# A two-layer float32 decoder trunk: the down projection's halves one group later, silu rows in the squares' buffers, rstd later in the first group

## The chip, the cores and the metric

The kernel runs on one core of a Trainium2 chip. A core has five engines that work side by side, each through its own instruction queue in order: TensorE (PE in the profile, with its weight loads as PEld) multiplies matrices, VectorE (DVE) and ScalarE (ACT) do elementwise work, GpSimd (POOL) does some more of it, and SyncE (SP) issues most DMAs. They wait for one another by semaphores. SBUF holds what the engines work on, PSUM the accumulating products, in eight banks. The metric is the device time of one execution in microseconds (us); less is better.

## The reference

The input is one sequence of 512 positions with 1024 features, all in float32. There are two layers. Each adds to the residual first a mixer and then a gated feed-forward block (FFN), both behind an RMS norm, and a last RMS norm follows. Layer 0's mixer is a short gated convolution beside a causal pooling over windows; layer 1's is a gated spatial mixing in chunks of 128 positions. The change lies in the two FFNs, which compute

```
def rms_norm(x, g):
    y = x * lax.rsqrt(jnp.mean(x * x, axis=-1, keepdims=True) + EPS)
    return y * g

def gated_conv_ffn(x, w_gate, w_up, conv_w, conv_b, w_down):
    g = x @ w_gate                       # 512 x 2816
    g = causal_dwconv3(g, conv_w) + conv_b
    up = x @ w_up                        # 512 x 2816
    return (silu(g) * up) @ w_down       # 512 x 1024

h = h + gated_conv_ffn(rms_norm(h, norm_ffn[layer]), ...)
```

## The kernel before

**Numbers in two parts.** Every float32 operand of a product is split into a part `hi` rounded to TensorE's float32r and the remainder `lo`, and a product is three: hi·hi, hi·lo, lo·hi (`mm3`, line 153). `hi` is a ScalarE copy. `lo` is made in one of two ways: by a VectorE subtraction (`halves`, line 677, and `parts`, line 146), or by a ScalarE copy of the negated source followed by a DMA from GpSimd's queue that adds the source onto it, beside the ScalarE copy that makes `hi` (`summed`, line 136, and lines 654 to 656).

**The rows of the FFN.** The 2816 hidden features are 22 tiles of 128 (`NF`). `Ffn.hidden(f)` makes tiles f and f+1 of silu(gate)·up. This text calls that a group; f is 0, 2, ..., 20. Group 0 multiplies directly (`direct`, line 604): 8 input tiles times 4 outputs (two gate, two up), three products of 512 columns each, 96 in all. The others use a seven-product block scheme for each of gate and up (`both`, line 681): fourteen products of twelve matmuls with 256 columns, on sums of blocks of the input (`block_sums`, line 634: `t41` and `t23` for each of four pairs `kp` of input tiles) and sums of blocks of the weights (`s12`, `s34`). The products g5 and u5, third and fifth in order, read `s12g` and `s12u`; they have the names g_4e and u_4e for group 4. The source tiles `t` of the block sums and the weight sums share one tag, "sum", with three buffers.

After a group, VectorE and ScalarE take its products out of PSUM, run the three-tap convolution (`conv`, line 573), silu (`silu`, line 582) and the product with `up`. The two finished rows `s` lie in a tag "s" with three buffers until `act` (line 587) splits them into a_hi and a_lo, a tag with four buffers each, so four rows can be split at a time.

**The down projection.** It runs in parts of two rows (the first) and then four, and each part in two halves of 512 output features. A half is `group` (line 158) with four PSUM banks: with `tail=4` the loop over outputs is the outer one for the last four rows, which for a part of four is all of it, so that the banks finish one after another; with `tail=0` the loop over rows is the outer one and all four banks finish in the last twelve products. VectorE adds each bank to the residual (line 310 in layer 0, whose weights and results have the name d; line 1099 in layer 1, name dn). The last part of layer 1 is `last_down` (line 1117), with the final norm.

**The order.** The list `STEPS` (line 523) says which halves follow which group, and whether the group's rows are split before (`late` False) or after them:

```
STEPS = [(0, False, []), (2, False, [(0, 2, 0), (0, 2, 1)]), (4, False, [(2, 6, 0)])]
for f in range(6, NF - 2, 4):
    STEPS += [(f, True, [(f - 4, f, 1)]), (f + 2, False, [(f, f + 4, 0)])]
```

So the first half of rows 2 to 5 follows group 4 directly, whose rows it reads. The program's order is a wish only: the framework's planner lays out every engine's queue at compile time. It takes what is ready by its own estimate of durations, earlier in the program first, and gives out buffers and waits. It can put products of the next group between those of a half. Instructions marked `inorder` keep the order in which the program names them.

**The norm.** The FFN multiplies the residual without its rstd, and the rstd is applied later. `Norm.square` (line 204) squares each residual tile on ScalarE into a tag "sq" with two buffers, and GpSimd adds it to `ssq`. In group 0, `rstd_cols` (line 223: eight small products ssc on TensorE, then square root, reciprocal and one refining step) and `rstd_spread` (line 213: four transposes ssr) are placed by counting (i, j), input tile and output, in the loop of `direct`: the first before the products of (1, 2), the second before those of (2, 1) (lines 770 and 772). In layer 1 the same loop also transposes the residual in its first two input tiles (`turn_residual`, line 1087).

**Weights.** A weight tile of 512 KB goes by SyncE's queue into a tag "raw" with four buffers; its parts lie in the tags "whi" and "wlo" with six buffers each, shared by all products.

Of the kernel before, what the change touches and what calls it, by code (L numbers as in the profile page):

```python
# [8 lines left out]
F32 = mybir.dt.float32  # L9
# [6 lines left out]
P = 128  # L16
D = 1024
S = 512
NK = D // P
NT = S // P  # L20
FF = 2816
NF = FF // P
# [10 lines left out]
def tile_trunk(ctx: ExitStack, tc: tile.TileContext, x, norm_mix, norm_ffn, final_norm,  # L33
# [9 lines left out]
    tp = ctx.enter_context(tc.tile_pool(name="tp", bufs=2))  # L43
# [3 lines left out]
    def mm_bank(name):  # L47
        return ps_mm.tile([P, 512], F32, tag="mm", name=name)
# [47 lines left out]
    def params(layer, rows_):  # L96
        return params_fetch(layer, rows_, nc.sync)()
# [55 lines left out]
    def mm3(ps, lhs, rhs, start, stop):  # L153
        nc.tensor.matmul(ps, lhs[0], rhs[0], start=start, stop=False)  # L154
        nc.tensor.matmul(ps, lhs[0], rhs[1], start=False, stop=False)  # L155
        nc.tensor.matmul(ps, lhs[1], rhs[0], start=False, stop=stop)  # L156

    def group(name, outs, ks, lhs, rhs, tail, on_done, before=None, at_end=None, begun=None):

        start, banks = begun or (0, {})
        head = max(0, len(ks) - tail)
        order = [(i, j) for i in range(start, head) for j in outs]
        order += [(i, j) for j in outs for i in range(head, len(ks))]
        at = start - 1
        for i, j in order:
            if i > at and before is not None:
                before(ks[i])  # L170
            at = max(at, i)
            if j not in banks:
                banks[j] = mm_bank(f"{name}_{j}")
            mm3(banks[j], lhs(ks[i], j), rhs(ks[i], j), i == 0, i == len(ks) - 1)
            if i == len(ks) - 1 and at_end is None:
                on_done(j, banks[j])
        if at_end is not None:
            at_end()
            for j in outs:
                on_done(j, banks[j])  # L180
# [114 lines left out]
            chunks[k0], chunks[k0 + 1] = (hi, lo, 0), (hi, lo, 1)  # L295
        return chunks

    def project(name, w, acts, ks, norm, before=None, halves=(0, 1)):

        for gi in halves:  # L300
            chunks = half_weights(name, w, ks, gi)

            def lhs(k, j):
                hi, lo, n = chunks[k]
                cs = slice(j * P, (j + 1) * P)
                return hi[:, n, cs], lo[:, n, cs]

            def done(j, ps):
                k = gi * 4 + j
                nc.vector.tensor_tensor(h[k], ps, h[k], ALU.add)  # L310
                if norm is not None:
                    norm.add(k)

            group(f"{name}{gi}", range(4), ks, lhs, lambda k, j: acts[k], 4, done,
                  before if gi == 0 else None)


# [202 lines left out]

    STEPS = [(0, False, []), (2, False, [(0, 2, 0), (0, 2, 1)]), (4, False, [(2, 6, 0)])]
    for f in range(6, NF - 2, 4):
        STEPS += [(f, True, [(f - 4, f, 1)]), (f + 2, False, [(f, f + 4, 0)])]
    STEPS[-1][2].append((NF - 4, NF, 1))
    HALF = S // 2
    NP = NK // 2
    PAIRS = [k for i in range(NP) for k in (i, i + NP)]
# [25 lines left out]
    class Ffn:  # L555
# [24 lines left out]
            return c  # L580

        def silu(self, c, ft):
            s = self.ap.tile([P, S], F32, tag="s", bufs=3, name=f"s{self.layer}_{ft}")
            nc.scalar.activation(s, c, AF.Silu, bias=self.prm("bf", ft))  # L584
            return s

# [47 lines left out]
        def block_sums(self, kp):  # L634

            n, g1, h1 = f"{self.layer}_{kp}", self.prm("ffn", kp + NP), h[kp + NP]
            t = self.ap.tile([P, 4, HALF], F32, tag="sum", bufs=3, name=f"t{n}")
            b11, b12 = t[:, 2, :], t[:, 3, :]
            nc.scalar.activation(t[:, 2:, :], h[kp].rearrange("p (a b) -> p a b", a=2), AF.Copy,
                                 scale=self.prm("ffn", kp))  # L640
            nc.vector.scalar_tensor_tensor(t[:, 1, :], h1[:, HALF:], g1, b12, op0=ALU.mult,
                                           op1=ALU.subtract)
            nc.vector.tensor_tensor(t[:, 0, :], t[:, 1, :], b11, ALU.add)
            nc.vector.tensor_tensor(b12, b12, b11, ALU.subtract)
            nc.vector.scalar_tensor_tensor(b11, h1[:, :HALF], g1, t[:, 0, :], op0=ALU.mult,
                                           op1=ALU.subtract)
            self.t23[kp] = self.sums(kp)
            t41 = self.ap.tile([P, 2, 2, HALF], F32R, name=f"t41_{n}")
            self.t41[kp] = t41[:, 0], t41[:, 1]
            for (hi, lo), src in ((self.t41[kp], t[:, 2:, :]), (self.t23[kp], t[:, :2, :])):  # L650
                if kp < 2:
                    self.halves(hi, lo, src)
                    continue
                nc.scalar.activation(lo, src, AF.Copy, scale=-1.0)
                nc.gpsimd.dma_start(lo, src, accum_op=ALU.add)
                nc.scalar.activation(hi, src, AF.Copy)
# [132 lines left out]
    def ffn0(norm):  # L789
        nonlocal prm1  # L790
        with tc.tile_pool(name="f0", bufs=1) as ap:
            def sums(kp):
                return [ap.tile([P, 2, HALF], F32R, name=f"t23{i}_{kp}") for i in "hl"]

            ffn = Ffn(0, prm0, norm, ap, sums)
            nxt = None
            for f, late, down_parts in STEPS:
                acts = ffn.hidden(f)
                if not late:
                    acts()  # L800
                for a, b, half in down_parts:
                    if b == NF and half == 0:
                        prm1 = params1()
                        nxt = Norm("m1", lambda k: prm1("mix", k))
                    project(f"d0_{a}", w_ffn_down[0], ffn.acts, list(range(a, b)), nxt,
                            halves=(half,))
                if late:
                    acts()
            return nxt


# [264 lines left out]
    def ffn1(norm):  # L1076
        with tc.tile_pool(name="f1", bufs=1) as ap:
# [4 lines left out]
            ffn = Ffn(1, prm1, norm, ap, sums)  # L1082
            acts = ffn.acts
# [18 lines left out]
            def half_down(a, b, half):  # L1102
                ks, cs = list(range(a, b)), slice(half * 512, half * 512 + 512)
                chunks = half_weights(f"dn{a}", w_ffn_down[1], ks, half)

                def lhs(k, t):
                    ts_ = slice(t * P, (t + 1) * P)
                    return acts[k][0][:, ts_], acts[k][1][:, ts_]

                def rhs(k, t):  # L1110
                    hi, lo, n = chunks[k]
                    return hi[:, n, :], lo[:, n, :]

# [60 lines left out]
            for f, late, down_parts in STEPS:  # L1174
                splits = ffn.hidden(f, before=before)
                if not late:
                    splits()
                if f == NF - 2:
                    last_down(NF - 4, NF)
                    break  # L1180
                for part in down_parts:
                    half_down(*part)
                if late:
                    splits()

    def down(name, ks, pieces, lhs, rhs, on_done):

# [41 lines left out]
```

## Time and profile before

| what | value |
|---|---|
| time, median of 3 runs | 1006.11 us (1004.69 to 1008.41) |
| the profiled execution | 1007.67 us, its span 1006.0 us |
| TensorE busy | 986.7 us |
| VectorE busy | 773.1 us |
| ScalarE busy | 542.1 us |
| GpSimd busy | 102.4 us |
| mean granted TensorE clock | 0.995 |
| DMA | 125.10 MB, 124 GB/s over the span |

Times in the trace are counted from the start of the span. Group 0 of layer 0 begins at 146.50 us and its last down product ends at about 500 us; layer 1's FFN runs from 642.9 us to the end of the span. A row of the timeline gives start, duration, engine, line, operation, what is written from what, shape, count, and in square brackets how long the engine was idle before and for whom. A row of the waits gives who waited for whom, the total, how often, and the longest. A row of the stretches gives start and end, the length, each engine's busy time, and behind them the granted clock, DMA's share and its GB/s. The profile models the ends of matmuls, which overlap, so their rate is read from start to start.

### The profile page before, as it was taken

What the parts mean: (1) busy time and instruction counts of PE and PEld (TensorE: products, weight loads), DVE (VectorE), ACT (ScalarE), POOL (GpSimd) and SP (SyncE); (2) the same over time, 40 slices, a digit from 0 to 9 for tenths busy, and PEclk for the clock granted to TensorE, in tenths of its full rate; (3) what the DMA queues carried; (4) which work ended last, traced back from release to release, by engine and by line L of the source; (5) the groups of instructions that cost most, each with busy time, mean ns of one, the idle gap of its engine ahead of it and who ended that gap; (6) DMA issues with size and microseconds to landing.
All of it is one profiled execution on the core that took longest, in us unless ns stands there. A gap on an engine that the chain in (4) does not pass through costs nothing.

```text
span 1006.0 us, 15310 instructions
## 1 busy us (share of the span) xinstructions
PE 986.7 (98%) x6049; PEld 883.9 (88%) x6049; DVE 773.1 (77%) x1174; ACT 542.1 (54%) x816; POOL 102.4 (10%) x117
## 2 busy tenths in 40 slices
PE   9999999999999999999999999989999999999997
PEld 6788887998999999999888988879989999999995
DVE  6896457878987778886988665668877887778867
ACT  5623446645555455554568734575546546455444
POOL 2141122000000000000211001220000000000000
PEclk9999999999999999999999999999999999999999
DMA  7442225545455464554432513164555545555422
GB/s 243 130 145 83 85 84 126 126 127 147 126 134 139 127 147 125 138 136 126 126 105 79 178 59 105 43 144 109 147 146 128 151 121 137 136 146 148 112 78 83
DMA packets 85251, 125.10 MB, mean 124 GB/s; under 512 B 4180, under 2 KB 56124, under 8 KB 85180
## 3 DMA queue, kind: packets, MB, share of 16 engines
q1 hardware_dynamic: 76204, 98.24, 31.1%
q0 software_dynamic: 7056, 23.60, 13.2%
q10 hardware_dynamic: 1920, 2.30, 0.6%
q8 instruction: 47, 0.77, 0.3%
q14 instruction: 24, 0.20, 0.1%
HBM read 98.42 MB, written 2.10 MB: 100 GB/s over the span
## 4 chain that ended last, share of the span: by engine, by line
PE 71%; DVE 11%; DMA 6%; issue 4%; ACT 4%; POOL 1%; SPq 0%; ACTq 0%; POOLq 0%; DVEq 0%
PE dn L154 4%; PE dn L155 4%; PE dn L156 4%; PE d L154 3%; PE d L155 3%; PE d L156 3%; DMA raw_g<-in_w_ffn_gate_dram 2%; DMA wlo_u<-raw_u 2%; DVE c L578 2%; PE oo L156 1%; PE oo L154 1%; PE oo L155 1%; PE oe L155 1%; PE oe L154 1%; PE oe L156 1%
## 5 line engine op out<-in xcount | busy, mean ns | idle before, releaser
L154 PE MATMUL dn<-whi_dn,a_hi 128*128 128x512 f32 (+1 forms) x180 | 69.6, 386 | 1.3 <-ACT a_hi L261 1.3
L154 PE MATMUL d<-a_hi,whi_d 128*128 128x512 f32 x176 | 66.5, 393 | 3.0 <-ACT a_hi L261 2.9
L155 PE MATMUL dn<-wlo_dn,a_hi 128*128 128x512 f32 (+1 forms) x180 | 69.4, 385 | 0.0
L155 PE MATMUL d<-a_lo,whi_d 128*128 128x512 f32 x176 | 68.8, 391 | 0.0
L156 PE MATMUL d<-a_hi,wlo_d 128*128 128x512 f32 x176 | 68.5, 389 | 0.0
L156 PE MATMUL dn<-whi_dn,a_lo 128*128 128x512 f32 (+1 forms) x180 | 67.3, 384 | 0.0
L578 DVE SCALAR_TENSOR_TENSOR c<-rows,prm,c 128x512 f32<-128x512 f32 x88 | 63.4, 743 | 0.4 <-ACT c L576 0.4
L141 POOL DMA_DIRECT2D wlo_g<-raw_g x20 | 17.3, 867 | 370.3 <-ACT wlo_g L140 370.3
L261 ACT ACTIVATE a_hi<-s 128x512 fp32r<-128x512 f32 x44 | 27.3, 627 | 48.0 <-PE dn L155 21.3
L150 DVE TENSOR_TENSOR wlo_dn<-raw_dn,whi_dn 128x1024 fp32r<-128x1024 f32 x22 | 26.9, 1224 | 30.7 <-ACT whi_dn L149 30.7
L150 DVE TENSOR_TENSOR wlo_d<-raw_d,whi_d 128x1024 fp32r<-128x1024 f32 x22 | 26.8, 1223 | 27.4 <-ACT whi_d L149 27.4
L154 PEld LDWEIGHTS d<-a_hi,whi_d 128*128 128x128 f32 x176 | 32.7, 188 | 10.3 <-ACT a_hi L261 4.0
L154 PEld LDWEIGHTS dn<-whi_dn,a_hi 128*128 128x128 f32 x180 | 33.9, 188 | 8.1 <-ACT a_hi L261 1.8
L141 POOL DMA_DIRECT2D wlo_u<-raw_u x21 | 18.1, 861 | 223.5 <-ACT wlo_u L140 137.2
L679 DVE TENSOR_TENSOR wlo_s34u<-s34u,whi_s34u 128x1024 fp32r<-128x1024 f32 x20 | 24.5, 1224 | 21.1 <-ACT whi_s34u L678 21.1
L156 PEld LDWEIGHTS dn<-whi_dn,a_lo 128*128 128x128 f32 x180 | 33.8, 188 | 7.0 <-DVE a_lo L263 0.2
L1099 DVE SCALAR_TENSOR_TENSOR y<-dn,small,y 128x512 f32<-128x512 f32 (+1 forms) x49 | 35.6, 734 | 5.6 <-PE dn L156 5.4
L155 PEld LDWEIGHTS dn<-wlo_dn,a_hi 128*128 128x128 f32 x180 | 33.9, 188 | 6.2
L149 ACT ACTIVATE whi_dn<-raw_dn 128x1024 fp32r<-128x1024 f32 x22 | 23.3, 1058 | 29.6 <-issue 2.6
L156 PEld LDWEIGHTS d<-a_hi,wlo_d 128*128 128x128 f32 x176 | 33.0, 188 | 6.8
L584 ACT ACTIVATE s<-c,prm 128x512 f32<-128x512 f32 x44 | 31.3, 717 | 13.7 <-DVE c L578 13.6
L155 PEld LDWEIGHTS d<-a_lo,whi_d 128*128 128x128 f32 x176 | 33.1, 188 | 6.4
(1377 smaller groups left out, 3568.8 us busy)
## 6 DMA issues: line engine op xcount, KB each, us to landing
raw_g<-in_w_ffn_gate_dram SPq DMA_DIRECT2D x40, 512.0 KB, 3.8
raw_u<-in_w_ffn_up_dram SPq DMA_DIRECT2D x40, 512.0 KB, 3.7
raw_d<-in_w_ffn_down_dram SPq DMA_DIRECT2D x22, 512.0 KB, 3.7
raw_dn<-in_w_ffn_down_dram SPq DMA_DIRECT2D x22, 512.0 KB, 3.6
wlo_u<-raw_u POOLq DMA_DIRECT2D x21, 512.0 KB, 5.4
wlo_g<-raw_g POOLq DMA_DIRECT2D x20, 512.0 KB, 4.8
raw_oe<-in_w_out_even_dram SPq DMA_DIRECT2D x8, 512.0 KB, 3.6
raw_v<-in_w_in_odd_dram SPq DMA_DIRECT2D x8, 512.0 KB, 4.9
```

The lines of the kernel that those rows point to most:

```text
L141: nc.gpsimd.dma_start(lo, raw, accum_op=ALU.add)
L149: behind(nc.scalar.activation(hi, raw, AF.Copy), after[1])
L150: behind(nc.vector.tensor_tensor(lo, raw, hi.bitcast(F32), ALU.subtract), after[0])
L154: nc.tensor.matmul(ps, lhs[0], rhs[0], start=start, stop=False)
L155: nc.tensor.matmul(ps, lhs[0], rhs[1], start=False, stop=False)
L156: nc.tensor.matmul(ps, lhs[1], rhs[0], start=False, stop=stop)
L261: nc.scalar.activation(hi, src, AF.Copy, scale=scale)
L578: nc.vector.scalar_tensor_tensor(c, t[:, i : S + i], prm("cf", i * NF + ft), c, op0=ALU.mult, op1=ALU.add)
L584: nc.scalar.activation(s, c, AF.Silu, bias=self.prm("bf", ft))
L679: nc.vector.tensor_tensor(lo, src, hi.bitcast(F32), ALU.subtract)
L1099: nc.vector.scalar_tensor_tensor(dst, ps, ffn.cols[:, t : t + 1], dst, op0=ALU.mult, op1=ALU.add)
```

## The change

Four things change, in both FFNs.

- A new method `steps` goes through a new `STEPS`: each entry has a group, at most one half that follows it, and the groups whose rows are split behind that half. Halves of rows f-4 to f-1 now follow groups f and f+2; the two halves of rows 0 and 1 follow groups 2 and 4. The rows of groups f and f+2 are split together behind the second of the halves. The last part (rows 18 to 21) follows in one piece, in layer 0 as `d0_last` with both halves, in layer 1 as `last_down`.
- The halves in `steps` have `tail=0`; `d0_last` keeps 4.
- Rows with an even number go into the tag "sq" (two buffers) instead of "s".
- In group 0 `rstd_cols` moves to (3, 0) and `rstd_spread` to (4, 1). In `block_sums` the pairs 0 and 1, not 2 and 3, get `lo` by GpSimd's DMA.

```
-    STEPS = [(0, False, []), (2, False, [(0, 2, 0), (0, 2, 1)]), (4, False, [(2, 6, 0)])]
-    for f in range(6, NF - 2, 4):
-        STEPS += [(f, True, [(f - 4, f, 1)]), (f + 2, False, [(f, f + 4, 0)])]
-    STEPS[-1][2].append((NF - 4, NF, 1))
+    STEPS = [(0, None, [0]), (2, (0, 2, 0), [2]), (4, (0, 2, 1), [4])]
+    for f in range(6, NF, 4):
+        STEPS += [(f, (f - 4, f, 0), []), (f + 2, (f - 4, f, 1), [f, f + 2])]
...
-            s = self.ap.tile([P, S], F32, tag="s", bufs=3, name=f"s{self.layer}_{ft}")
+            name = f"s{self.layer}_{ft}"
+            s = (self.ap.tile([P, S], F32, tag="s", bufs=3, name=name) if ft % 2 else
+                 tp.tile([P, S], F32, tag="sq", name=name))
...
-                if kp < 2:
+                if kp > 1:
                     self.halves(hi, lo, src)
                     continue
...
-                    if (i, j) == (1, 2):
+                    if (i, j) == (3, 0):
                         nc.vector.tensor_copy(self.cols, self.norm.rstd_cols(inorder))
-                    elif (i, j) == (2, 1):
+                    elif (i, j) == (4, 1):
                         self.r = self.norm.rstd_spread(inorder)
...
+        def steps(self, half_down, before=lambda i, j: None):
+            waiting = {}
+            for f, part, ready in STEPS:
+                waiting[f] = self.hidden(f, before)
+                if part is not None:
+                    half_down(*part)
+                for done in ready:
+                    waiting[done]()
...
+            def half_down(a, b, half):
+                project(f"d0_{a}", w_ffn_down[0], ffn.acts, list(range(a, b)), None,
+                        halves=(half,), tail=0)
+
+            ffn.steps(half_down)
+            prm1 = params1()
+            nxt = Norm("m1", lambda k: prm1("mix", k))
+            project("d0_last", w_ffn_down[0], ffn.acts, list(range(NF - 4, NF)), nxt)
             return nxt
...
-                group(f"dn{a}_{half}", range(NT), ks, lhs, rhs, 4,
+                group(f"dn{a}_{half}", range(NT), ks, lhs, rhs, 0,
                       lambda t, ps: add(y[t][:, cs], ps, t))
...
+            ffn.steps(half_down, before)
+            last_down(NF - 4, NF)
```

More of the change, by code (lines that the diff above doesn't have):

```diff
@@ L296, in half_weights, with project @@
         return chunks
-    def project(name, w, acts, ks, norm, before=None, halves=(0, 1)):
+    def project(name, w, acts, ks, norm, before=None, halves=(0, 1), tail=4):
         for gi in halves:
@@ L312, in done @@
                     norm.add(k)
-            group(f"{name}{gi}", range(4), ks, lhs, lambda k, j: acts[k], 4, done,
+            group(f"{name}{gi}", range(4), ks, lhs, lambda k, j: acts[k], tail, done,
                   before if gi == 0 else None)
@@ L795, in ffn0 @@
             ffn = Ffn(0, prm0, norm, ap, sums)
[L796 to L808, printed above, removed]
+            def half_down(a, b, half):
[5 more added lines that the diff above has]
+            project("d0_last", w_ffn_down[0], ffn.acts, list(range(NF - 4, NF)), nxt)
             return nxt
@@ L1172, in last_down @@
                 down(f"dn{a}", list(range(a, b)), pieces, lhs, rhs, done)
[L1174 to L1184, printed above, removed]
+            ffn.steps(half_down, before)
+            last_down(NF - 4, NF)
     def down(name, ks, pieces, lhs, rhs, on_done):
```

## The prediction

> **What bounds the kernel now.** I read the busy line of the profile's page first, then stretches cut at the places the change touches, then what TensorE waited for. From the profile's page:
>
> ```profile
> span 1006.0 us, 15310 instructions
> PE 986.7 (98%) x6049; PEld 883.9 (88%) x6049; DVE 773.1 (77%) x1174; ACT 542.1 (54%) x816; POOL 102.4 (10%) x117
> ```
>
> TensorE is busy 98% of the span, so the change, which removes no product, can only win some of 19.3 us of idle time and whatever time TensorE runs slow. The stretches (start:end, length, then busy time per engine; the granted clock follows POOL) show where that lies:
>
> ```profile
> 146.50:194.36 47.86, 45.68 (x277) 40.75 (x276) 38.85 (x69) 32.45 (x50) 8.75 (x8) 0.96 0.46 110
> 194.36:205.27 10.91, 10.91 (x51) 9.02 (x49) 10.91 (x21) 4.40 (x7) 0.85 (x1) 1.00 0.41 98
> 231.29:500.50 269.21, 266.19 (x1802) 247.15 (x1801) 220.47 (x330) 145.43 (x214) 19.91 (x19) 1.00 0.51 134
> 642.90:694.97 52.07, 49.02 (x310) 44.16 (x308) 38.53 (x66) 37.34 (x61) 7.53 (x8) 0.97 0.43 101
> 731.81:976.40 244.59, 243.32 (x1705) 228.82 (x1704) 190.22 (x283) 129.91 (x193) 12.90 (x15) 1.00 0.51 132
> ```
>
> In the long regular part of each FFN (third and fifth row) TensorE idles 3.0 and 1.3 us. The entry of each FFN (first and fourth) idles 2.2 and 3.1 us and has a clock below 1. The second row is two halves of the first down projection, 48 products in 10.91 us, 0.227 us each; VectorE is busy in all of it. TensorE's waits name the causes (total, times, longest):
>
> ```profile
> PE d L154 <- ACT a_hi L261: 2.9, 3, 2.3
> PE u_2e L544 <- DVE wlo_s12u L679: 2.1, 1, 2.1
> PE ssc_f L227 <- POOL ssq_f L210: 1.9, 1, 1.9
> PE dn L154 <- ACT a_hi L261: 1.3, 1, 1.3
> PE ssr_f L217 <- DVE rc_f1c L251: 0.9, 1, 0.9
> ```
>
> All five are waits that the change is about. They add up to 9.1 us, and two have a tail in the clock, cut here into windows of 3.41 us:
>
> ```profile
> 149.88:153.29 3.41, 1.50 (x10) 1.02 (x8) 3.00 (x4) 2.19 (x3) 3.33 (x2) 1.00 0.00 0
> 153.29:156.71 3.42, 3.42 (x11) 2.84 (x11) 2.71 (x11) 2.01 (x4) 0.25 (x1) 0.50 0.80 153
> 231.80:235.21 3.41, 2.04 (x18) 1.84 (x16) 3.41 (x8) 1.92 (x3) 0.00 (x0) 1.00 0.10 19
> 675.53:678.94 3.41, 1.31 (x11) 1.31 (x12) 2.74 (x5) 3.38 (x5) 0.86 (x1) 1.00 0.64 123
> 678.94:682.36 3.42, 3.42 (x19) 3.42 (x18) 3.16 (x5) 2.40 (x5) 0.00 (x0) 0.50 0.40 76
> ```
>
> After windows in which TensorE was busy 1.50 and 1.31 us the next one ran at clock 0.50; after one with 2.04 it did not. The Trainium skill ("TensorE: Matmul & The Clock Gate", Part 1) asks for about 3.4 us of idleness before the clock halves; here 1.9 to 2.1 us sufficed, so trace and page differ and I go by the trace. The same section calls these windows free-running; the two halved ones start 525.65 us apart, 154 times 3.413, which agrees. The price of a halved window: products that start every 0.227 us took 3.02 us for seven,
>
> ```profile
> 153.82 0.77 PE L154 MATMUL gu<-hgh,whi_u 128*128 128x512 f32 x1
> ...
> 156.84 0.40 PE L155 MATMUL gu<-hgl,whi_g 128*128 128x512 f32 x1
> ```
>
> so 3.02 - 7 x 0.227 = 1.4 us.
>
> **The change, part by part.**
>
> *rstd later, layer 0.* The column sums (ssc) stand after 18 products, and wait for GpSimd's last addition to ssq:
>
> ```profile
> 149.96 2.64 POOL L210 TENSOR_TENSOR ssq_f<-ssq_f,sq_f 128x512 f32<-128x512 f32 x1 [2.57 <-DVE t L643]
> 152.65 1.31 PE L227 MATMUL ssc_f<-small,ssq_f 128*128 128x1 f32 x8 [1.91 <-POOL ssq_f L210]
> ```
>
> Placed after 36 products they come 18 x 0.227 = 4.1 us later, at about 154.7, when ssq (152.6) is there. Gain: 1.9 of wait and 1.4 of halved clock, 3.3.
>
> *rstd later, layer 1.* There the sums don't wait, but the spread (ssr) waits 0.93 us for the chain ssc, square root, reciprocal:
>
> ```profile
> 650.14 0.95 PE L227 MATMUL ssc_f<-small,ssq_f 128*128 128x1 f32 x8
> 652.66 1.28 ACT L241 ACT_TABLE_LOAD   x1
> 655.10 0.62 PE L217 MATMUL ssr_f<-ident,rc_f1c 128*128 128x128 f32 x4 [0.93 <-DVE rc_f1c L251]
> ```
>
> The chain takes 4.0 us from the end of ssc. Between the new places stand five groups of three products, 15 x 0.227 = 3.4 us; it is covered but for 0.6 us at most, and ScalarE no longer copies transposed residuals in it. I take 0.9 gained and 0.3 lost for both layers (bounds 0 and 1.2).
>
> *Block sums: the first two pairs, not the last two, get their low parts from GpSimd's DMA.* Per pair the one way takes two ScalarE and two VectorE instructions, the other four ScalarE and two DMAs from GpSimd's queue; the totals stay. The source tile has three buffers shared with the weight sums, so VectorE waits for the last pairs' DMAs:
>
> ```profile
> 166.79 0.69 DVE L709 TENSOR_TENSOR s34g<-raw_g 128x512 f32<-128x512 f32 x1 [3.43 <-DMA t<-t]
> 665.34 0.69 DVE L709 TENSOR_TENSOR s34g<-raw_g 128x512 f32<-128x512 f32 x1 [1.66 <-DMA t<-t]
> 676.35 1.22 DVE L679 TENSOR_TENSOR wlo_s12u<-s12u,whi_s12u 128x1024 fp32r<-128x1024 f32 x1
> t<-t POOLq DMA_DIRECT2D x6, 256.0 KB, 5.1
> ```
>
> Issued some 8 us sooner, behind the ssq addition, these DMAs (5.1 us to landing) hold up the fourth pair's buffer and the first weight sum instead, from about 152.6 to 159, and the later weight sums wait for two splits on the engines alone. VectorE regains 3.4 us in layer 0 and 1.7 or more in layer 1. TensorE's 2.1 us wait for wlo_s12u in layer 1 and its halved window go: 3.5. Lost, at least 0. GpSimd's queue is the one they are moved past:
>
> ```profile
> 152.54 1.00 POOL L141 DMA_DIRECT2D wlo_g<-raw_g  x1
> 164.14 0.85 POOL L655 DMA_DIRECT2D t<-t  x1 [0.19 <-issue]
> ```
>
> The weight DMA that they may now precede is read only in group 2, after the 96 products of group 0 (21.8 us), so four issues of 0.85 don't show. If they came ahead of the ssq addition, it would end at 152.6 + 3.4 = 156.0 and ssc wait 1.3; I take 0, as the square is ready before the block sums are.
>
> *Halves one group further back.* A half now reads activations that were split a whole group (14 x 1.44 = 20.2 us by the chain's row below) earlier, so the waits for a_hi go: 2.9 + 1.3 = 4.2.
>
> ```profile
> 305.19 1.44 PE g_10e L544 x12
> L261 ACT ACTIVATE a_hi<-s 128x512 fp32r<-128x512 f32 x44 | 27.3, 627 | 48.0 <-PE dn L155 21.3
> ```
>
> A group's evacuation, for which a_hi waited, now runs beside a half (5.4 us at the front, 10.9 later) and the next group.
>
> The price is at the front. Between group 2 and group 4 stood both halves of the first down part; now one, 24 products, so TensorE arrives 5.4 us sooner where VectorE is full and wlo_s12u was in time by nothing:
>
> ```profile
> 202.74 3.07 DVE L310 TENSOR_TENSOR h<-d,h 128x512 f32<-128x512 f32 x5
> 210.41 1.22 DVE L679 TENSOR_TENSOR wlo_s12u<-s12u,whi_s12u 128x1024 fp32r<-128x1024 f32 x1
> 211.26 0.28 PE L544 MATMUL g_4b<-hgh,whi_g 128*128 128x256 f32 x1
> 211.69 0.39 PE L544 MATMUL u_4e<-t,wlo_s12u 128*128 128x256 f32 x1
> ```
>
> VectorE drops four of these additions (0.6 us from start to start), 2.4: the shortfall is 5.4 - 2.4 = 3.0 per site, at groups 4 and 6 of both layers, 12 at most. At least it is 0. SyncE's queue fetched both halves' weights ahead of group 4's,
>
> ```profile
> 167.51 1.02 SPq L130 DMA_DIRECT2D raw_d<-in_w_ffn_down_dram  x2
> 186.33 0.37 SPq L130 DMA_DIRECT2D raw_u<-in_w_ffn_up_dram  x1
> ```
>
> and now fetches the second half's behind them: each of group 4's four takes the buffer of the one before, so VectorE can sum them sooner. And the planner fills holes with other products, as with g_4b at 211.26, where 0.43 went by for 0.12. That 0.3 is the nearest row, though for a smaller shortfall; I take 0.8 per site, 3.2. If no such cover is left, the end of 12 holds.
>
> *Waiting rows and four splits at once.* Two rows wait in the squares' buffers, which nothing else uses between group 0 and the last part: no cost. Every second group has four splits ahead of it instead of two: two more a_lo, 1.2 us of VectorE before wlo_s12u. The slack there:
>
> ```profile
> 305.37 1.22 DVE L679 TENSOR_TENSOR wlo_s12u<-s12u,whi_s12u 128x1024 fp32r<-128x1024 f32 x1
> 308.15 0.28 PE L544 MATMUL u_10e<-t,wlo_s12u 128*128 128x256 f32 x1
> ```
>
> is 1.6 us. The residual additions now come four together at a half's end (k is the outer loop, tail=0), 2.4 us. Bounds 0 and 3 x (1.2 + 2.4 - 1.6) = 6.0 for layer 0's groups 10, 14 and 18. VectorE idled 1.6 us between the spaced additions, which it now can use, so I take 0.3.
>
> *Last part of each layer.* The splits of the last rows need buffers that the half before them frees k by k, the last one at its end; then 0.63 (a_hi) and 0.68 (a_lo). Two earlier k of four banks, 24 products, cover it: 0, at most 1.3 per layer.
>
> **Sum.** Gains 3.3 + 0.9 + 3.5 + 4.2 = 11.9; losses 0.3 + 3.2 + 0.3 = 3.8; net -8.1. The profiled execution took 1007.67 us (span 1006.0), 1.56 above the median 1006.11: 999.6 for such a one, 998.0 for the median.
>
> **The rivals.** (a) *The front holds and the whole gain comes*: 1006.1 - 11.9 = 994.2. For it: group 4's weights come sooner and the planner has the second half's 24 products to put in a hole; against it: their weights are then prepared late, by the same full VectorE. (b) *The halved windows stay*: by the trace the idle time in the window counts, but only two cases carry this; if the waits don't cause the halving, 2 x 1.4 stays: 1000.8. By the Trainium skill's page above ("TensorE: Matmul & The Clock Gate") it goes this way, since no wait here is near 3 us, and the sum would be -5.3. (c) *The bunched VectorE work bites in the regular part*: 6.0 instead of 0.3 and the front as forecast: 1003.7. Against it: layer 1 has neither L755 nor L759 and more slack. (d) *Slower: TensorE outruns VectorE at the front.* At all four sites nothing fills the hole, 3.0 each, and every wait halves the next window, 1.4: 17.6 lost, with 0.6 elsewhere 1006.1 - 11.9 + 18.2 = 1012.4. It decides once a site costs over 11.3 / 4 = 2.8. For it: VectorE is busy through all of 194.36:205.27 and in-order; against it: fetches move up and at 211 the order did fill.
>
> **How the numbers follow.** Forecast 0.50 (994.5 to 1001), (a) 0.14, (b) 0.08, (c) 0.12, (d) 0.16. What a measurement can tell from no change is about 0.5%, 5 us. Faster by that (below 1001.1): forecast, (a) and part of (b), 0.67; within: (c) and the rest of (b), 0.16; slower 0.17, (d) and a little more. The range 991 to 1009 reaches below (a) by 3, since bounds of 0 were taken as they stand, and above (c) by 5, where (d) comes with two or three of its four sites; the whole of (d) is left out.
>
> **What would show it.** Right: no wait of ssc for ssq, none of d or dn for a_hi, none of u_2e over 0.5; clock 1.00 from 146 to 700; s34g not behind DMA t; groups of the regular part at 20.2 + 10.9 = 31.1 us each with a half. Wrong: u_4e or u_6e waiting over 3 us for wlo_s12u, a window at clock 0.50 after it, VectorE without gaps from group 2 to 8, or TensorE waiting for banks behind the additions.

## The result and the profile after

| | before | after |
|---|---|---|
| median, us | 1005.78 (1004.69 to 1008.41) | 994.65 (993.93 to 995.35) |
| profiled execution, us | 1007.67 | 993.98 |
| its span, us | 1006.0 | 992.2 |

The median before is of four runs here, the three of the table ahead and one more. The ratio is 0.9885, with a 95% interval of 0.9864 to 0.9907. The kernel is 11.1 us faster; the forecast was 8.1 us, 998.0. The time came out 3.3 us below the forecast, inside the range given and at the edge of the forecast's own 994.5 to 1001, and within 0.5 us of rival (a), 994.2. The forecast's sum was partly right by luck, as the parts below show: errors of several us cancelled.

The busy lines of the page of the changed kernel, and then all that TensorE waited for (total, times, longest):

```profile
span 992.2 us, 15316 instructions
PE 980.7 (99%) x6049; PEld 880.9 (89%) x6049; DVE 769.4 (78%) x1174; ACT 544.6 (55%) x816; POOL 99.1 (10%) x117
```

```profile
PE ssr_f L217 <- DVE rc_f0c L251: 2.3, 1, 2.3
PE clock L62 <- DVE idle L57: 1.3, 1, 1.3
PE ssr_f L217 <- DVE rc_f1c L251: 0.8, 1, 0.8
```

The waits for a_hi, for ssq and for wlo_s12u are gone, and so are two of 0.5 and 0.3 us in layer 1's mixer that the prediction had not touched. One wait is new and the largest: ssr in layer 0, 2.3 us. In layer 1 ssr waits as before. (The wait named clock is at the start of the kernel and stands in both profiles.)

The stretches of the changed kernel (start:end, length, busy times, granted clock behind POOL): the entry of layer 0's FFN, its front (from the first down product to group 8), the rest of that FFN; then the entry of layer 1's FFN, its front, and the rest up to the last down product:

```profile
146.49:192.50 46.01, 43.74 (x278) 39.42 (x276) 41.05 (x72) 32.62 (x51) 9.06 (x9) 1.00 0.49 116
192.50:254.65 62.15, 62.15 (x435) 58.34 (x433) 57.61 (x92) 37.26 (x56) 3.81 (x5) 1.00 0.55 147
254.65:494.20 239.55, 239.55 (x1611) 222.18 (x1609) 193.16 (x289) 130.94 (x191) 17.66 (x18) 1.00 0.50 134
635.13:683.51 48.38, 47.54 (x309) 42.78 (x308) 39.96 (x69) 37.64 (x60) 8.33 (x9) 1.00 0.47 111
683.51:745.66 62.15, 62.15 (x435) 58.34 (x433) 55.99 (x88) 37.41 (x55) 4.31 (x5) 1.00 0.59 151
745.66:984.92 239.26, 239.26 (x1621) 222.62 (x1619) 184.25 (x293) 126.71 (x195) 10.33 (x12) 1.00 0.46 124
```

Behind the entries the profile shows no idle time of TensorE: its busy time is the length of the stretch in four rows of six, and the clock is 1.00 in all. The same parts of the kernel before, layer 0's front, the rest of layer 0, and layer 1 from behind its entry to its last down product, show where 2.5, 0.7 and 1.3 us of idle time stood:

```profile
194.36:270.42 76.06, 73.59 (x483) 67.45 (x482) 66.06 (x104) 40.19 (x59) 4.29 (x5) 1.00 0.50 132
270.42:500.58 230.16, 229.47 (x1562) 213.47 (x1561) 186.13 (x278) 124.94 (x185) 18.19 (x17) 1.00 0.51 135
694.97:998.54 303.57, 302.25 (x2054) 280.98 (x2052) 242.45 (x382) 162.98 (x250) 15.48 (x18) 1.00 0.48 127
```

(The front of before is longer by 48 down products, 10.9 us, which now come later; front and rest are compared as a sum.) Cut at the same events, the two profiled executions differ so:

| stretch | before | after | gained | forecast |
|---|---|---|---|---|
| layer 0: entry | 47.87 | 46.01 | 1.86 | 3.15 |
| layer 0: front, rest, last part | 306.22 | 301.70 | 4.52 | 1.0 |
| layer 1's mixer | 142.36 | 140.93 | 1.43 | 0 |
| layer 1: entry | 52.03 | 48.38 | 3.65 | 4.25 |
| layer 1: front, rest, last part | 303.57 | 301.41 | 2.16 | -0.3 |

The column of the forecast puts the prediction's terms where they belong: 3.3 less half of the 0.3 for ssr; 2.9 of a_hi less two sites of 0.8 and the 0.3 for bunched work; 0.9 and 3.5 less the other half; 1.3 less two sites. It adds up to 8.1, the gains measured to 13.6. By the medians 11.1 are left, since the profiled execution of before was 1.9 above its median and that of after 0.7 below.

### The profile page after: what moved, and what is told of

Same layout as the page of the kernel before. It is cut to its first block, busy times and chain, and to the rows that moved or that the text cites. A ratio compares the mean times of both kernels' runs of the same rounds, so it can differ in the third digit from the quotient of the medians.

```text
span 992.2 us, 15316 instructions
## 1 busy us (share of the span) xinstructions
PE 980.7 (99%) x6049; PEld 880.9 (89%) x6049; DVE 769.4 (78%) x1174; ACT 544.6 (55%) x816; POOL 99.1 (10%) x117
## 4 chain that ended last, share of the span: by engine, by line
PE 92%; DVE 2%; ACT 1%; issue 1%; DMA 0%; POOL 0%; ACTq 0%; DVEq 0%
PE dn L154 4%; PE dn L156 4%; PE dn L155 4%; PE d L155 3%; PE d L154 3%; PE d L156 3%; PE v L154 1%; PE oo L154 1%; PE oo L155 1%; PE v L155 1%; PE v L156 1%; PE oo L156 1%; PE oe L155 1%; PE oe L154 1%; PE oe L156 1%; PE g_2a L543 1%
## 5 line engine op out<-in xcount | busy, mean ns | idle before, releaser
L154 PE MATMUL d<-a_hi,whi_d 128*128 128x512 f32 x144 | 56.1, 390 | 0.0
L155 PE MATMUL d<-a_lo,whi_d 128*128 128x512 f32 x144 | 56.1, 390 | 0.0
L156 PE MATMUL d<-a_hi,wlo_d 128*128 128x512 f32 x144 | 56.0, 389 | 0.0
L143 ACT ACTIVATE whi_u<-raw_u 128x1024 fp32r<-128x1024 f32 x21 | 22.1, 1054 | 30.7 <-PE d L155 16.5
L150 DVE TENSOR_TENSOR wlo_d<-raw_d,whi_d 128x1024 fp32r<-128x1024 f32 x18 | 22.0, 1223 | 19.9 <-ACT whi_d L149 19.9
L199 ACT ACTIVATE hgh<-h,prm 128x512 fp32r<-128x512 f32 x24 | 17.3, 722 | 33.3 <-DVE h L310 33.2
L210 POOL TENSOR_TENSOR ssq_f<-ssq_f,sq_f 128x512 f32<-128x512 f32 x14 | 19.7, 1411 | 144.1 <-ACT sq_f L209 109.2
```

The source lines that it names most:

```text
L143: behind(nc.scalar.activation(hi, raw, AF.Copy), first)
L150: behind(nc.vector.tensor_tensor(lo, raw, hi.bitcast(F32), ALU.subtract), after[0])
```

## The experiments

The theory at first was the prediction's own: each part has its own stalls to remove, and the front costs something. The rivals: one part carries the whole gain, or the parts hand their stalls to one another. All kernels compute the whole of the reference. Medians and ratios are against runs of the kernel before on the same chip; the first four runs of the table were on one chip, the others on a second, where the changed kernel's own median is 994.03.

| run | median, us | ratio to before (95%) | span, us |
|---|---|---|---|
| rstd later, alone | 1001.79 | 0.9959 (0.9945 to 0.9974) | 1000.7 |
| block sums, alone | 1006.90 | 0.9996 (0.9976 to 1.0016) | 1005.5 |
| halves and rows, alone | 999.77 | 0.9941 (0.9918 to 0.9964) | 996.3 |
| the change, rstd's spread at (5, 1) | 994.33 | 0.9887 (0.9864 to 0.9910) | 993.1 |
| the change, block sums undone | 993.76 | 0.9875 (0.9854 to 0.9897) | 992.2 |
| the change, second half's weights ahead | 998.92 | 0.9923 (0.9895 to 0.9950) | 997.2 |
| the change, outer loop over outputs | 996.94 | 0.9907 (0.9886 to 0.9929) | 995.3 |
| spread at (5, 1), products reordered | 998.74 | 0.9926 (0.9904 to 0.9947) | 996.9 |
| spread at (5, 1) in layer 0 only | 992.75 | 0.9862 (0.9836 to 0.9889) | 991.2 |
| the changed kernel again | 994.03 | 0.9880 (0.9856 to 0.9904) | 993.6 |

### The three parts, one at a time

rstd alone, in the kernel before:

```
-                    if (i, j) == (1, 2):
+                    if (i, j) == (3, 0):
...
-                    elif (i, j) == (2, 1):
+                    elif (i, j) == (4, 1):
```

> The kernel before with only the two rstd places moved, (1, 2) to (3, 0) and (2, 1) to (4, 1). Theory (the prediction's term): layer 0's 1.9 us wait of ssc and its halved clock window (1.4) go, and layer 1's 0.93 us wait of ssr; with the block sums as before nothing in VectorE's queue waits for a DMA inside the rstd chain, so ssr waits under 0.6 in both layers: 4.0 us faster than before, 3 to 5. Rival (the halved window isn't the wait's doing): clock 0.50 still stands near 153, and the gain is 2 to 3 us. The 2.1 us wait of u_2e in layer 1 stays in either.

The block sums alone:

```
-                if kp < 2:
+                if kp > 1:
```

> The kernel before with only the block sums changed (pairs 0 and 1 by GpSimd's DMA). Theory: the 2.1 us wait of u_2e in layer 1 and its halved window go, 3.5 us. If the new 2.3 us wait of ssr in the changed kernel comes from VectorE's s12g waiting for a DMA ahead of the rstd chain, part of it shows here too, 0 to 2 us, so 1.5 to 3.5 us faster. Rival (the wait of u_2e has another cause, the evacuation of group 0 on VectorE): u_2e still waits over 1 us and the time is that of before.

The order of halves and the place of the waiting rows alone: the change with these two edits taken back.

```
-                if kp > 1:
+                if kp < 2:
...
-                    if (i, j) == (3, 0):
+                    if (i, j) == (1, 2):
...
-                    elif (i, j) == (4, 1):
+                    elif (i, j) == (2, 1):
```

> The changed kernel with the block sums and the rstd places as before: only the halves one group later, tail=0, and the rows in the squares' buffers. Theory A (front for nothing, since group 4's weights come sooner): every a_hi wait goes, 4.2 us and some 0.6 of smaller ones, 4 to 5 us faster than before. Theory B (the prediction's front price of 3.2 us, hidden in the changed kernel by the other two parts, which let VectorE run ahead): u_4e or u_6e waits 0.5 to 3 us and the gain is 1 to 2.5 us.

The waits of TensorE with rstd alone:

```profile
PE d L154 <- ACT a_hi L261: 2.3, 1, 2.3
PE u_2e L544 <- DVE wlo_s12u L679: 1.4, 2, 0.9
...
PE ssr_f L217 <- DVE rc_f0c L251: 0.6, 1, 0.6
PE v L154 <- ACT v L960: 0.6, 1, 0.6
PE ssr_f L217 <- DVE rc_f1c L251: 0.5, 1, 0.5
```

With the block sums alone:

```profile
PE d L154 <- ACT a_hi L261: 3.1, 2, 2.9
PE dn L154 <- ACT a_hi L261: 2.5, 1, 2.5
...
PE u_4e L544 <- DVE kept L742: 1.2, 1, 1.2
```

With halves and rows alone:

```profile
PE u_2e L543 <- DVE wlo_s12u L680: 2.3, 1, 2.3
PE ssc_f L227 <- POOL ssq_f L210: 1.9, 1, 1.9
```

Three readings follow. First, moving rstd by itself takes the ssc wait away, and, against what was expected, it also cuts the 2.1 us wait for wlo_s12u in layer 1, which the prediction had given to the block sums, to 0.9 (layer 0 has a new one of 0.5): the entries shrink from 47.87 to 45.37 and from 52.03 to 49.30 us. Its cover is as forecast: ssr waits 0.6 and 0.5. In layer 0 a window of halved clock now follows the a_hi wait of 2.3 us, which no such window followed in the prediction's trace; the last section shows why that can change. Second, the block sums by themselves shorten the entries as much (to 45.09 and 49.01 us), but the time does not move: what lies behind them grows by 1.0 us in layer 0 and 4.5 in layer 1, where the a_hi wait is 2.5 us, a window of halved clock follows it, and a new wait of 1.2 us for kept stands. The reading is that TensorE came sooner to a front that VectorE and ScalarE set; it is argued from these waits, not tested by itself. Third, with halves and rows alone every a_hi wait and the two of the mixer are gone, while the waits of the entries stand as in the kernel before. Only the halved window behind the ssc wait is missing, as the edge of a window cuts that wait in two. The gain of 6.1 us is more than its theory had (4 to 5). Singly the parts give 4.1, -1.0 and 6.1 us, 9.2 in all; together 11.1. The likely reason for the difference is that with the first two the gain of an entry could be lost again at the front, and the new order leaves no wait there to be lost to.

### What holds the entry: the place of the spread, and the block sums

The new wait of ssr: layer 0's entry of the changed kernel, VectorE's and GpSimd's instructions around it, and TensorE's transposes ssr.

```profile
155.29 1.20 POOL L656 DMA_DIRECT2D t<-t  x1
...
158.53 0.15 DVE L243 TENSOR_TENSOR ms_f0c<-ms_f0c,rc_f0c 128x4 f32<-128x4 f32 x1
160.12 0.69 DVE L699 TENSOR_TENSOR s12g<-raw_g,raw_g 128x512 f32<-128x512 f32 x1 [1.44 <-issue]
160.73 0.15 DVE L244 SCALAR_TENSOR_TENSOR ms_f0c<-ms_f0c,rc_f0c 128x4 f32<-128x4 f32 x1
...
161.14 0.15 DVE L251 SCALAR_TENSOR_TENSOR rc_f0c<-ms_f0c,rc_f0c 128x4 f32<-128x4 f32 x1
...
161.44 0.62 PE L217 MATMUL ssr_f<-ident,rc_f0c 128*128 128x128 f32 x4 [2.27 <-DVE rc_f0c L251]
```

Lines 244 and 251 are the last two steps of the chain to rstd, 0.15 us each; they could follow line 243 at 158.7. In front of them in VectorE's queue stands the first weight sum, s12g, and it does not start until 160.12. The view names no releaser, but the semaphores in the trace do: s12g waits from 158.28 for the fourth of the DMAs of t, issued at 155.29, whose last part lands at 160.05 (the tiles share a tag of three buffers). So a wait that has nothing to do with rstd sits in the middle of its chain. If that is the cause, the change with the block sums undone must have a short ssr wait:

```
-                if kp > 1:
+                if kp < 2:
```

> The changed kernel with the block sums as before (pairs 2 and 3 by GpSimd's DMA). The prediction's term: their change is worth 3.5 us by the wait of u_2e in layer 1 and its halved window, so 998 here. New theory from the first four runs (the entry of an FFN ends when VectorE has made wlo_s12u, and a wait taken away ahead of it only comes back at u_2e): the entries come out as in the kernel with the rstd places alone, 45.4 and 49.3 us against 46.0 and 48.4 in the changed kernel, so within 1 us of it, 994 to 996; the wait of ssr falls from 2.3 to under 0.9 in layer 0, since VectorE no longer waits for a DMA inside the rstd chain, and u_2e waits 0.5 to 1.2 in its place.

VectorE and TensorE at the same place of that run:

```profile
158.73 0.68 DVE L699 TENSOR_TENSOR s12g<-raw_g,raw_g 128x512 f32<-128x512 f32 x1
159.33 0.15 DVE L251 SCALAR_TENSOR_TENSOR rc_f0c<-ms_f0c,rc_f0c 128x4 f32<-128x4 f32 x1
...
159.63 0.62 PE L217 MATMUL ssr_f<-ident,rc_f0c 128*128 128x128 f32 x4 [0.64 <-DVE rc_f0c L251]
```

s12g does not wait and ssr waits 0.64 instead of 2.27 (0.5 in layer 1), and the entries are 45.37 and 49.12 us, as expected. But the gain is taken back a little later, where TensorE waits for VectorE's wlo_s12u in both layers:

```profile
PE u_2e L543 <- DVE wlo_s12u L680: 1.3, 2, 0.7
```

The span is 992.2 us as with the change whole. Beside the other two parts, the block sums' edit is worth nothing: it trades 0.7 us before each wlo_s12u for a longer wait of ssr.

The other way to shorten the wait is to ask for rstd later:

```
-                    elif (i, j) == (4, 1):
+                    elif (i, j) == (5, 1):
```

> The changed kernel with rstd_spread at (5, 1) instead of (4, 1), four more groups of three products (2.7 us) between ssc and ssr. Theory (the chain ssc to rstd is 5 to 6 us long in the changed kernel, its cover 3.4): the waits of ssr, 2.3 and 0.8 us, both go, 3 us less than the changed kernel, near 991, and with no wait over 1.4 us left the halved window that half of the changed kernel's runs show doesn't come, so its runs lie within 0.7 us. Rival (the chain is pushed back with it, as VectorE's order is laid out anew): ssr still waits over 1 us and the time stays at 994 to 995.

The ssr waits went, but the time did not fall to 991; TensorE waited for wlo_s12u instead:

```profile
PE u_2e L543 <- DVE wlo_s12u L680: 2.9, 2, 2.0
```

The two layers answer differently. In layer 0 the entry is 44.94 us against 46.01, the wait there 0.9. In layer 1 it is 50.87 against 48.38: the wait there is 2.0 us, and a window of clock 0.50 follows it. So the spread was moved in layer 0 only, beside the changed kernel itself on the same chip:

```
-                    elif (i, j) == (4, 1):
+                    elif (i, j) == (5 if self.layer == 0 else 4, 1):
```

> The change with the spread of rstd one step later still, at (5, 1), in layer 0 only; layer 1 keeps (4, 1). Theory (the stalls of the entries belong to the places, one by one): layer 0 takes the entry of the run with both places later (44.94 us where the changed kernel has 46.01) and layer 1 keeps its own (48.38 against 50.87 there), so the span falls by about 1.1 us, to about 991.1, and the time to about 993. Rival (the loss only changes its place): the L0 wait for ssr of 2.3 us is replaced by one for VectorE's second-half sums (0.9 us there), a halved clock window turns up (1.4 us), and the time is that of the changed kernel on the same chip within 0.5 us, or above it.

> The changed kernel itself, beside the run with layer 0's spread moved, on the same chip. Both theories: its times stand in two groups about 1.4 us apart, near 993.9 and 995.3, as its first four did; the upper group is the one with a granted clock below full speed for one window in layer 0's entry.

The two entries of the run with the spread later in layer 0, and its waits:

```profile
146.51:191.39 44.88, 43.84 (x278) 39.55 (x277) 40.89 (x72) 32.73 (x51) 9.07 (x9) 1.00 0.50 119
634.02:682.41 48.39, 47.55 (x309) 42.73 (x308) 39.96 (x69) 37.66 (x60) 8.35 (x9) 1.00 0.46 111
```

```profile
PE u_2e L543 <- DVE wlo_s12u L680: 0.9, 1, 0.9
PE ssr_f L217 <- DVE rc_f1c L251: 0.8, 1, 0.8
```

The entries are 44.88 and 48.39 us, as the theory had them, and 992.75 us (992.53 to 992.99) is below every one of the changed kernel's five runs there (993.88 to 995.36). It beats both kernels, the changed one by 1.3 us only. All four of these kernels (the changed one, block sums undone, the spread later in both layers and in layer 0 only) end within 2 us of one another: in an entry some 1 to 2 us of VectorE's delay stays, and the edits choose which wait shows it.

One more attempt on layer 1: the spread at (5, 1) in both layers, and the products that read wlo_s12u later in every group.

```
-            for key, product in (("g", 1), ("u", 1), ("g", 5), ("g", 6), ("u", 5), ("u", 6),
-                                 ("g", 2), ("g", 7), ("u", 2), ("u", 7), ("g", 4), ("g", 3),
+            for key, product in (("g", 1), ("u", 1), ("g", 5), ("g", 6), ("g", 2), ("g", 7),
+                                 ("u", 5), ("u", 6), ("u", 2), ("u", 7), ("g", 4), ("g", 3),
```

> The changed kernel with rstd_spread at (5, 1), and in every group the products g2 and g7 ahead of u5 and u6, so that u5 reads wlo_s12u two products (2.9 us) later. Theory (entry set by wlo_s12u): with neither ssr nor u5 early, the waits of 1.1 and 2.2 us that the kernel with the spread alone later showed at u_2e go, and its halved window (1.4) with them: entries near 43.9 and 47.3 us, 989 to 991 in all. Rival (VectorE and ScalarE are full there, and another operand is late instead): TensorE waits as long at another product and the time stays at 993 to 995.

This failed: it is 4 us slower than the changed kernel. In the entries TensorE's waits only changed their names, once more:

```profile
PE g_2a L543 <- ACT rows L733: 1.3, 1, 1.3
...
PE u_2b L543 <- DMA wlo_u<-raw_u: 1.0, 1, 1.0
```

The larger part of the loss lies where there was nothing to win: the rest of layer 0 takes 241.50 us (239.55 after) and layer 1's groups 8 to 20 take 208.24 (206.39), while TensorE counts as busy in nearly all of it. This loss is the edit's own. Products 6 and 7 share a PSUM bank (`BANK`, bank a), and ScalarE copies product 6 out of it at line 733 before product 7 may write there. Three products stood between the two; the new order leaves one, 1.44 us. ScalarE's copy of u6 and the first products of u7 in group 10:

```profile
298.21 0.35 ACT L733 COPY kept<-u_10a 128x256 f32<-128x256 f32 x1
298.62 0.39 PE L543 MATMUL u_10a<-t23h,whi_s34u 128*128 128x256 f32 x1
298.84 0.28 PE L543 MATMUL u_10a<-t23l,whi_s34u 128*128 128x256 f32 x1
```

u7 begins only when the copy is done, and its first two products start 0.22 us apart, where the changed kernel has 0.12. From start to start, such steps at g7 and u7 (0.10 to 0.16 us, once 0.7) add up to 2.0 us in the one stretch and 1.9 in the other, which is the loss; the list of waits shows only the largest, 0.4 us at g_8a. So this run does not test a later u5 alone.

### Why the front cost nothing: the order of fetching

The prediction put 0.8 us at each of four sites of the front, with bounds 0 and 3.0. Measured were 0: both fronts take 62.15 us, with no idle time. The DMA issues in SyncE's queue that fetch group 4's weights, the last weight split that group 4 waited for in the kernel before, and its first reader, in the changed kernel:

```profile
166.32 0.37 SPq L130 DMA_DIRECT2D raw_g<-in_w_ffn_gate_dram  x1
...
183.02 0.37 SPq L130 DMA_DIRECT2D raw_u<-in_w_ffn_up_dram  x1
187.19 0.37 SPq L130 DMA_DIRECT2D raw_d<-in_w_ffn_down_dram  x1
...
202.48 1.21 DVE L680 TENSOR_TENSOR wlo_s12u<-s12u,whi_s12u 128x1024 fp32r<-128x1024 f32 x1
...
204.20 0.28 PE L543 MATMUL u_4e<-t,wlo_s12u 128*128 128x256 f32 x1
```

In the kernel before the four stood behind the two raw_d, and the last of them was issued at 186.33; now the second raw_d is behind them. u_4e reads wlo_s12u 7.5 us sooner (204.20 against 211.69), and VectorE starts on it 7.9 us sooner (202.48 against 210.41): 0.5 us to spare. (1.9 us of both is the shorter entry.) To see whether the fetch does this, the second half's weights of rows 0 and 1 were fetched and split ahead of group 4's again, with all else as changed:

```
-            chunks = half_weights(name, w, ks, gi)
+            chunks = made.pop((name, gi), None) or half_weights(name, w, ks, gi)
...
+                if (a, half) == (0, 0):
+                    made["d0_0", 1] = half_weights("d0_0", w_ffn_down[0], [0, 1], 1)
...
+                if (a, half) == (0, 0):
+                    made["dn0", 1] = half_weights("dn0", w_ffn_down[1], [0, 1], 1)
```

> The changed kernel, but the weights of the second half of rows 0 and 1 are fetched and split ahead of group 4's weights in the program, as before the change. Theory (the front cost nothing because group 4's raw weights landed 3 to 6 us sooner): u_4e waits 1 to 3 us for wlo_s12u in both layers, perhaps with a halved window, and the time is 996 to 1001. Rival (four fewer residual additions on VectorE were enough by themselves): no wait over 0.5 at u_4e, within 0.5 us of the changed kernel.

SyncE's queue, the split of s12g and its reader in this run:

```profile
163.74 2.72 SPq L130 DMA_DIRECT2D raw_d<-in_w_ffn_down_dram  x2
168.99 0.37 SPq L130 DMA_DIRECT2D raw_g<-in_w_ffn_gate_dram  x1
180.31 0.37 SPq L130 DMA_DIRECT2D raw_u<-in_w_ffn_up_dram  x1
...
203.23 1.22 DVE L682 TENSOR_TENSOR wlo_s12g<-s12g,whi_s12g 128x1024 fp32r<-128x1024 f32 x1
...
204.50 0.39 PE L545 MATMUL g_4e<-t,wlo_s12g 128*128 128x256 f32 x1 [1.54 <-DVE wlo_s12g L682]
```

Its front in layer 0:

```profile
193.88:258.65 64.77, 62.99 (x435) 58.57 (x434) 59.95 (x96) 37.77 (x56) 4.74 (x6) 1.00 0.52 141
```

It grew from 62.15 us to 64.77, and layer 1's to 63.37: 2.6 and 1.2, together 3.8 us. (The spans differ by 5.0 us; a window of halved clock in layer 0's entry, 1.6, is more than the rest. The changed kernel run again has such a window too, and its front is still 62.15.) The waits came at other products than the theory named: in layer 0 at g_4e, not u_4e, and in layer 1 the listed wait is of g_4a for ScalarE's rows, 0.7. So the place of these weights, ahead of group 4's or behind them, decides whether the front is free. Fetch and split moved together here: VectorE makes one split wlo_d more (1.2 us) ahead of s12g, and then idles 0.7 and 0.6 us until raw_g and raw_u land; which of the two weighs more wasn't separated. The prediction's 3.2 is near what the front costs when the weights come as late as before, though the waits stand at group 4 of each layer only, not at its four sites.

### The outer loop of the halves

```
-                        halves=(half,), tail=0)
+                        halves=(half,), tail=4)
...
-                group(f"dn{a}_{half}", range(NT), ks, lhs, rhs, 0,
+                group(f"dn{a}_{half}", range(NT), ks, lhs, rhs, 4,
```

> The changed kernel with tail=4 in the halves, so that the banks of a half finish one after another and none of its four rows is done with before the half's end. If the loop order is of no account in the regular part: no wait of d or dn there, regular parts as in the changed kernel. What it may cost: the four splits behind a half find their buffers only at its end, so the first down products of the last part wait 0 to 3 us for a_hi in each layer, and the four splits fall together with the preparation of the next group. 994 to 999.

With the loop over outputs outside again the median rose by 2.3 us; but its profiled execution has a halved window in layer 0's entry, which some runs of the changed kernel have as well. Against those (995.3) 1.5 to 1.6 us remain: 0.46 and 0.41 in layer 0's front and rest, 0.18 and 0.50 in layer 1's. Four residual additions in one bunch, which the prediction priced at 0.3 against the change, are no loss here. That spaced additions cost more by themselves is not shown, as this edit also moves the moment when the rows' buffers come free.

## Why the prediction was right and wrong

*What bounds the kernel.* Right. No product was removed and the gain is idle time of TensorE and halved clock: the listed waits of TensorE are 4.4 us where those of before were 11.6.

*rstd later, layer 0: 3.3.* The mechanism was right: ssc no longer waits and the halved window is gone. The 1.4 us of the window was in part luck: with halves and rows alone the same 1.9 us wait stands and halves nothing. *rstd later, both layers: 0.9 and -0.3.* The term "I take 0.9 gained and 0.3 lost for both layers (bounds 0 and 1.2)" failed: ssr waits 2.3 us in layer 0 and 0.8 in layer 1, 3.1 in all and outside the bounds. Two steps are in it. The chain was taken as 4.0 us of its own work, but its steps of 0.15 us stand in VectorE's queue in order, among instructions of other work: from the end of ssc to ssr it took 5.8 us in layer 0 and 4.9 in layer 1. And the prediction saw that the DMAs of t would now hold up "the first weight sum instead, from about 152.6 to 159", but did not ask what stood behind that sum. With the block sums undone ssr waits 0.6 and 0.5, which is what the prediction had as its most.

*Block sums: 3.5.* The 2.1 us wait and the halved window in layer 1 are gone, but they were put down to one part that was not needed for it. Either edit alone shortens that wait; the sums alone bring nothing to the time, and undone beside the rest they cost nothing. The halved window goes already when rstd alone brings the wait from 2.1 to at most 0.9.

*Halves one group further back: 4.2.* Right in mechanism, low in size. From start to start, the products before a_hi stood off by 2.5, 0.5, 0.4 and 0.25 us beyond their rate in layer 0 and 1.4 in layer 1, 5.1 in all, and all of it went.

*The front: -3.2.* Mis-sized: 0. The argument that SyncE's queue would now bring group 4's weights sooner stood in the prediction, as a reason for the lower end; the run with these weights ahead again bears it out, and the value was taken from a hole of 0.3 us that belonged to the old fetch order. Counted from the first down product, VectorE came to wlo_s12u not 2.4 but 6.1 us sooner, and TensorE 5.6.

*Bunched VectorE work: -0.3.* 0: the regular parts show no idle time of TensorE, and the run with spaced additions is not faster.

*Not seen: layer 1's mixer, 1.4.* Its waits for v and u (0.5 and 0.3 us) stand with rstd alone and with the sums alone, and are gone with halves and rows alone, so they belong to that part. Through which instructions, the runs do not tell.

*The rivals.* (a) came by the time, and its condition held: the front cost nothing. Its sum did not: ssr still waited 3.1 us, and the mixer's 1.4 and stalls too small for the list of waits stood against that. (b) fell: with the waits of ssc and u_2e their halved windows went. But the sign "clock 1.00 from 146 to 700" holds in five of the changed kernel's nine runs only, since the new wait of ssr halves a window in the others. (c) and (d) fell with the stretches above.

## What to carry to other kernels

Before pricing a move, list what stands behind the moved instruction in each in-order queue: a 0.15 us step of a chain can inherit a DMA's wait through an instruction ahead of it that it does not need. Where one engine sets the pace of a stretch, several small waits of another engine are one delay under several names; sum the stretch, and do not add the waits up as gains. When an order of work changes, read first where the weights' fetches and splits fall, since they can move the preparation by more than the work itself was moved. And when products are reordered, count what is left between two that share a PSUM bank.

## What the runs showed of the hardware

The same wait costs 1.4 us more or not, by where it falls. The changed kernel's nine runs stand in two groups, five at 993.88 to 994.03 and four at 995.32 to 995.36. Two consecutive windows of 3.41 us around the wait of ssr in layer 0, in the run of the first group that was profiled:

```profile
157.44:160.86 3.42, 1.73 (x8) 1.10 (x6) 1.86 (x7) 1.53 (x3) 0.85 (x1) 1.00 0.76 131
160.86:164.27 3.41, 2.83 (x15) 2.43 (x16) 3.41 (x10) 2.56 (x4) 0.00 (x0) 1.00 0.73 139
```

In one of the second group:

```profile
158.44:161.85 3.41, 1.12 (x8) 0.73 (x7) 1.97 (x8) 0.96 (x2) 0.85 (x1) 1.00 0.73 133
161.85:165.27 3.42, 3.42 (x10) 2.67 (x9) 3.42 (x6) 3.01 (x4) 0.00 (x0) 0.50 0.42 88
```

The wait is 2.3 us in both. In the first the edge of a window cuts it in two, TensorE is busy 1.73 us in the window that has the larger part of the wait, and the clock stays; in the second it lies in one window, TensorE is busy 1.12 us of it, and the next window runs at 0.50. The run with the spread at (5, 1) in both layers has one more such window, ahead of its halved one:

```profile
663.78:667.19 3.41, 1.40 (x12) 1.20 (x11) 3.21 (x5) 3.38 (x4) 0.86 (x1) 1.00 0.43 105
```

With the prediction's rows, busy times up to 1.50 us of 3.41 halved the next window, and 1.73 or more did not; the edge lies somewhere between, near half. No window of the two FFNs in the other kept traces speaks against it. So a wait of about 2 us has a chance of a halved window, not a fixed price: the kernel before, with several such waits, ran in 1002.78 us at a mean clock of 0.998 and in up to 1010.08 at 0.992, while the kernel with the spread later in layer 0, whose longest wait in the FFNs is 0.9, stayed within 0.5 us. The Trainium skill ("TensorE: Matmul & The Clock Gate", Part 1) says that the window is free-running and that the phase varies from run to run, which these two groups agree with; that the clock halves after an idle window of about 3.4 us does not agree with them, as TensorE was busy for up to 1.50 us of the windows that halved it.
